# Stick-breaking heads without a mask in the logits: ones in the running product, ones and zeros on the weights

## The chip, the cores and the metric

The kernel runs on one core of a Trainium2 chip. The metric is the device time of one execution in microseconds: three runs of the kernel before took 705.34, 706.74 and 708.4 us, so its median is 706.74 us. Five engines work side by side, each on its own list of instructions in a fixed order: TensorE (PE: matmuls, whose stationary operand is loaded by PEld), VectorE (DVE), ScalarE (ACT), GpSimd (POOL) and SyncE (SP, which issues DMAs). An engine that waits for another holds up all that stands behind the waiting instruction on its own list.

## The reference

One decoder layer on 512 tokens of width 1024: an attention stage with two kinds of heads, a gated feed-forward stage with a short convolution, a gated embedding stage, and a last norm. The change concerns the eight stick-breaking heads, each of width 64:

```
past  = key_pos < q_pos                                  # strictly earlier keys
z     = (q @ k.T) * scale
log_not = where(past, log_sigmoid(-z), 0)
between = reverse_cumsum(log_not) - log_not              # keys between s and t
w     = where(past, exp(log_sigmoid(z) + between), 0)    # weight of key s for query t
out   = w @ v
```

So a weight is sigmoid(z) times the product of sigmoid(-z) over the later keys that the query sees. Keys that it doesn't see must count as 1 in the product and as 0 in the weights.

## The kernel before

Tokens lie in four blocks of 128 queries. Every projection is computed in three matmuls of 512 columns (`mm3`, lines 121 to 123) from operands that are split into a high and a low part; ACT makes the high part of a weight tile (`whi`, line 140) and DVE the low one (`wlo`, line 141). The attention stage takes the stick-breaking heads in four pairs, pair 0 to pair 3, and then the four differential heads. A generator for each pair yields between its steps, and a table `plan` in `stages` says how many units of projection work (three matmuls each) PE does between one step of a pair and the next. These units are the cover under which DVE and ACT work on the pair. PE's order is the order in which the code is written; ACT, DVE and POOL are ordered by a scheduler, by priorities and its own estimates.

A pair's logits fill three PSUM tiles `z`, called groups here by the `g` of `sb_sticks`: group 0 holds query block 3 (512 keys), group 1 blocks 2 and 0 (384 and 128 keys), group 2 block 1 (256 keys), each for both heads. `logits` (line 482) writes them, and at line 490 adds -1e30 at unseen keys of the diagonal block by a matmul of the identity with a mask, two per group. `sb_sticks` then has ACT write sigmoid(-z) into `cum` (line 514) and sigmoid(z) into `beta` (line 515); DVE runs the product backwards over the keys (the scan, line 521) and multiplies `beta` with it (line 522). Because of the mask, sigmoid(-z) is 1 and sigmoid(z) is 0 at unseen keys. The second operand of the scan, `fresh`, has a 1 where a new row of keys begins: the maximum with it starts the product anew.

`pair_out` then transposes the weights block by block on PE (line 566), into which the weights of all three groups go, the first block being one of group 2. Two engines split the result (lines 535 and 536), and PE multiplies with the values (line 578). Between these steps DVE also has: `qkt` (line 377), which evicts a projection from PSUM, the low parts `q` and `k` (line 379), `wlo`, and in pair 1 the values' low part `v_sb` (line 501), which frees the four PSUM buffers `mm` of the value projection. Of `mm` there are four buffers, of `z` two.

Of the kernel before, what the change touches and what calls it, by code (L numbers as in the profile page):

```python
# [11 lines left out]
F32 = mybir.dt.float32  # L12
F32R = mybir.dt.float32r
AF = mybir.ActivationFunctionType
ALU = mybir.AluOpType
# [3 lines left out]
P = 128  # L19
T = 512  # L20
# [13 lines left out]
NEG = -1e30  # L34
# [7 lines left out]
class Kern:  # L42
# [121 lines left out]
    def consts(self):  # L164
        nc, a = self.nc, self.a
        c = self.cpool = self.open("consts")
        self.small = self.open("small", bufs=2)
        self.wraw = self.open("wraw", bufs=2)
        self.wsp = self.open("wsp", bufs=3)
        self.dram = self.open("dram", space=DRAM)  # L170
        su = self.su = self.open("setup", side="right")

        nc.scalar.preload_act_table_set("natural_log_exp_and_others")
        self.ident = c.tile([P, P], F32, name="ident")
        make_identity(nc, self.ident)
        self.ones = c.tile([P, P], F32, name="ones")
        nc.gpsimd.memset(self.ones, 1.0)
        self.mhalf = c.tile([P, 8], F32, name="mhalf")
        nc.gpsimd.memset(self.mhalf, -0.5)
        self.identR = c.tile([P, P], F32R, name="identR")  # L180
        nc.vector.tensor_copy(self.identR, self.ident)
        zero = su.tile([P, P], F32, name="zero")
        nc.gpsimd.memset(zero, 0.0)
        msk = su.tile([P, P], F32, name="msk")

        nc.gpsimd.affine_select(msk, zero, pattern=[[-1, P]], compare_op=ALU.is_gt, fill=NEG, base=0, channel_multiplier=1)
        self.maskR = c.tile([P, P], F32R, name="maskR")
        nc.vector.tensor_copy(self.maskR, msk)

    def params_attn(self, pst):  # L190
        nc, c = self.nc, self.cpool
# [277 lines left out]
            self.nc.vector.tensor_add(self.hT[nt], ps, self.hT[nt])  # L469


    def logits(self, q, k, blocks, mask=False):


        nc = self.nc
        z = self.psz()
        for at, (tb, col) in enumerate(blocks):
            n = (tb + 1) * P
            for i, (x, y) in enumerate(((0, 1), (1, 0), (0, 0))):
                for h in range(2):  # L480
                    o = slice(h * HD, (h + 1) * HD)
                    nc.tensor.matmul(  # L482
                        z[:, h, col : col + n], lhsT=q[o, x, tb * P : (tb + 1) * P], rhs=k[o, y, :n],
                        start=i == 0 and at == 0, stop=i == 2 and at == len(blocks) - 1 and not mask, skip_group_check=True,
                    )
        if mask:

            d = [col // P + tb for tb, col in blocks]
            for h in range(2):
                nc.tensor.matmul(  # L490
                    z[:, h, :].rearrange("p (a b) -> p a b", b=P)[:, d[0] : d[-1] + 1, :], lhsT=self.identR,
                    rhs=self.maskR.unsqueeze(1).to_broadcast([P, len(d), P]), start=False, stop=True, skip_group_check=True,
                )
        return z

    def evict_v(self, tb, ps):
# [7 lines left out]
    def sb_sticks(self, z, g):  # L504


        nc = self.nc
        w = 2 * P if g == 2 else T
        n = 2 * w
        beta = self.slot("beta", "wc" if g == 2 else "w")  # L510
        c = self.cum[g % 2]
        off = 2 * T - n
        two = lambda t: t.rearrange("p (a b) -> p a b", a=2)
        nc.scalar.activation(two(c[:, off : 2 * T]), z[:, :, :w], AF.Sigmoid, scale=-1.0)  # L514
        nc.scalar.activation(two(beta), z[:, :, :w], AF.Sigmoid)

        for c0 in range(off, 2 * T, T):
            back = c[:, c0 : c0 + T][:, ::-1]
            r0 = (3 - g) * P
            fresh = self.fresh[:, r0 : r0 + T] if g else self.fresh[:, 0:1].to_broadcast([P, T])  # L520
            nc.vector.tensor_tensor_scan(back, back, fresh, 1.0, op0=ALU.mult, op1=ALU.max)  # L521
        nc.vector.tensor_mul(beta, beta, c[:, off + 1 : 2 * T + 1])
        for h in range(2):
            b = beta[:, h * w : (h + 1) * w]
            if g == 0:
                self.at[h, 3] = b
            elif g == 1:
                self.at[h, 2], self.at[h, 0] = b[:, : 3 * P], b[:, 3 * P :]
            else:
                self.at[h, 1] = b  # L530
# [8 lines left out]
    def pair_steps(self, pair):  # L539

        q, k = self.qks.pop(pair)
        self.at = {}
        zs = [self.logits(q, k, ((3, 0),), True), self.logits(q, k, ((2, 0), (0, 3 * P)), True)]
        for g in range(2):
            self.sb_sticks(zs[g], g)
        yield
        self.sb_sticks(self.logits(q, k, ((1, 0),), True), 2)
        yield
        yield from self.pair_out(pair, self.v[0])

# [152 lines left out]
    def stages(self):  # L703
        nc, a, tc = self.nc, self.a, self.tc
# [20 lines left out]
        zs = [self.psz(), self.psz()]  # L725
# [66 lines left out]
        for t in self.cum:  # L792
            nc.gpsimd.memset(t[:, 2 * T :], 1.0)

        self.fresh = self.work.tile([P, 6 * P], F32, name="fresh", bufs=1)
        nc.gpsimd.memset(self.fresh, 0.0)
        nc.gpsimd.memset(self.fresh[:, 3 * P : 3 * P + 1], 1.0)
        self.v[0] = self.vp.tile([P, NB, 2 * T], F32R, tag="v", name="v_sb")

        for evict in self.late:  # L800
# [13 lines left out]
        for i in range(2):  # L814
            vd, b = self.vd[:, 2 * i : 2 * i + 2, :], slice(2 * i, 2 * i + 2)
# [66 lines left out]
        for n, (ft, gv) in enumerate(tiles):  # L882
            c, i = divmod(ft, 2)
# [66 lines left out]
        for nh in range(2):  # L950
# [11 lines left out]
            for tb in range(NB):  # L962
                last = nh == 1 and tb == NB - 1
                n = T // 2 if last else T
                for c0 in range(0, T, n):
                    cs = slice(c0, c0 + n)
                    ps = self.psm()[:, :n]
                    for k in range(KT):
                        w = tuple(x[:, k % 2, cs] for x in sp[k // 2])
# [4 lines left out]
                    h = h2n[tb][:, nh * T + c0 : nh * T + c0 + n]  # L974
# [60 lines left out]
```

## Time and profile before

| | |
|---|---|
| median of three runs | 706.74 us (705.34 to 708.4) |
| the profiled execution | 706.04 us, of which its span is 704.3 us |
| TensorE (PE) busy | 684.6 us, 97% of the span |
| VectorE (DVE) busy | 443.1 us, 63% |
| ScalarE (ACT) busy | 315.3 us, 45% |
| GpSimd (POOL) busy | 42.5 us, 6% |
| mean granted TensorE clock | 0.991 of 2.4 GHz |

The span is cut into instructions of each engine with their start and length. In a row of the timeline the first number is the start in us from the span's start, the second the length; "x6" merges six equal instructions, and the bracket at the end gives the time that the engine stood idle ahead of it and what ended that. Consecutive instructions overlap a little in the records, so the cost of one among others is read from start to start. A long matmul's record is longer than its share of PE's time for the same reason. The granted clock is 1.00 at 2.4 GHz and 0.50 at 1.2 GHz. Pair 0 lies at 38 to 62 us, pair 1 at 62 to 97, pair 2 at 102 to 128 and pair 3 at 130 to 156; the differential heads follow to about 240 us.

### The profile page before, as it was taken

How to read it: one execution, taken by the hardware profiler on the slowest of the kernel's cores; microseconds unless marked ns; L12 is line 12 of the kernel's file. 1: busy time of each engine (PE TensorE's matmuls, PEld its weight loads, DVE VectorE, ACT ScalarE, POOL GpSimd, SP SyncE). 2: the span in 40 equal slices, each digit the busy share in tenths (PEclk: the TensorE clock that was granted, in tenths of full speed). 3: DMA queues.
4: the chain of work that ended last, by engine and by line, in shares of the span. 5: the costliest groups of instructions: out<-in, count | busy, mean ns of one | idle time of the engine just before them, and what ended most of it. 6: DMA issues, size and time to landing. Idle time of an engine off the chain costs nothing. (4 is left out here: it accounts for less than half of the span.)

```text
span 704.3 us, 8234 instructions
## 1 busy us (share of the span) xinstructions
PE 684.6 (97%) x3263; PEld 561.2 (80%) x3263; DVE 443.1 (63%) x671; ACT 315.3 (45%) x465; POOL 42.5 (6%) x52
## 2 busy tenths in 40 slices
PE   7999999999999999999999999999999999999995
PEld 6777878787888887888888888888888888888885
DVE  5567669668676768498777777677734232437345
ACT  4565445556554543365444444444423232327422
POOL 2200000000100024100000000000000020202001
PEclk9899999999999999999999999999999999999998
DMA  9423135242226111223322233321323133127002
GB/s 285 158 74 99 60 111 189 60 118 80 76 87 210 60 60 61 87 93 121 119 72 91 77 120 119 95 85 60 126 98 105 60 104 120 41 95 252 17 27 93
DMA packets 66809, 71.64 MB, mean 102 GB/s; under 512 B 2360, under 2 KB 55850, under 8 KB 66771
## 3 DMA queue, kind: packets, MB, share of 16 engines
q1 hardware_dynamic: 63376, 64.76, 28.9%
q10 hardware_dynamic: 2755, 4.27, 1.7%
q0 software_dynamic: 640, 2.10, 0.8%
q8 instruction: 25, 0.41, 0.2%
q14 instruction: 13, 0.11, 0.0%
HBM read 66.90 MB, written 6.84 MB: 105 GB/s over the span
## 5 line engine op out<-in xcount | busy, mean ns | idle before, releaser
L140 ACT CAST whi<-wraw 128x1024 fp32r<-128x1024 f32 (+1 forms) x102 | 105.8, 1037 | 155.1 <-PE mm L122 125.1
L141 DVE TENSOR_TENSOR wlo<-wraw,whi 128x1024 fp32r<-128x1024 f32 (+1 forms) x102 | 123.5, 1211 | 75.0 <-ACT whi L140 73.8
L121 PE MATMUL mm<-xgh,whi 128*128 128x512 f32 x128 | 53.8, 420 | 1.5 <-ACT xgh L330 1.5
L122 PE MATMUL mm<-xgl,whi 128*128 128x512 f32 x128 | 51.5, 402 | 2.0 <-DVE xgl L331 2.0
L860 DVE TENSOR_TENSOR vpad<-mm,rb 128x512 f32<-128x512 f32 x44 | 30.1, 689 | 33.7 <-PE mm L123 33.6
L123 PE MATMUL mm<-xgh,wlo 128*128 128x512 f32 x128 | 51.0, 399 | 0.0
L689 POOL TENSOR_TENSOR sqacc<-sqacc,sq 128x512 f32<-128x512 f32 x14 | 23.1, 1652 | 359.0 <-issue 254.9
L862 ACT ACTIVATE y<-vpad,par,par 128x512 f32<-128x512 f32 x44 | 35.6, 816 | 2.7 <-DVE vpad L860 2.5
L864 DVE SCALAR_TENSOR_TENSOR y<-vpad,par,y 128x512 f32<-128x512 f32 x44 | 33.1, 752 | 1.3
L863 DVE SCALAR_TENSOR_TENSOR y<-vpad,par,y 128x512 f32<-128x512 f32 x44 | 32.8, 748 | 0.0
L121 PEld LDWEIGHTS mm<-xgh,whi 128*128 128x128 f32 x128 | 24.7, 193 | 8.1 <-ACT xgh L330 2.3
L122 PEld LDWEIGHTS mm<-xgl,whi 128*128 128x128 f32 x128 | 24.7, 193 | 8.0 <-DVE xgl L331 3.9
L866 ACT ACTIVATE y<-y 128x512 f32<-128x512 f32 x22 | 13.9, 633 | 34.9 <-DVE y L864 34.9
L123 PEld LDWEIGHTS mm<-xgh,wlo 128*128 128x128 f32 x128 | 24.6, 192 | 5.3
L521 DVE TENSOR_TENSOR_SCAN cum<-cum,fresh 128x512 f32<-128x512 f32 x20 | 23.6, 1213 | 5.5 <-ACT cum L514 5.5
L121 PE MATMUL mm<-whi,xgh 128*128 128x512 f32 x64 | 25.5, 398 | 0.0
L123 PE MATMUL mm<-whi,xgl 128*128 128x512 f32 x64 | 25.0, 390 | 0.0
L122 PE MATMUL mm<-wlo,xgh 128*128 128x512 f32 x64 | 25.0, 390 | 0.0
L626 ACT ACTIVATE pr<-pr,nmx 128x512 f32<-128x512 f32 (+3 forms) x32 | 17.7, 555 | 12.6 <-DVE nmx L622 12.4
L482 PE MATMUL z<-k,q 64*128 64x512 f32 (+3 forms) x192 | 20.3, 335 | 2.8 <-DVE k L379 1.7
L482 PEld LDWEIGHTS z<-k,q 64*128 64x128 f32 x192 | 15.2, 185 | 8.5 <-issue 4.6
L536 DVE TENSOR_TENSOR twl<-z,twh 128x1024 fp32r<-128x1024 f32 (+2 forms) x20 | 18.5, 953 | 5.2 <-ACT twh L535 5.0
(537 smaller groups left out, 1762.9 us busy)
## 6 DMA issues: line engine op xcount, KB each, us to landing
wraw<-in_w_up SPq DMA_DIRECT2D x22, 1024.0 KB, 5.1
wraw<-in_w_in SPq DMA_DIRECT2D x16, 512.0 KB, 5.2
wraw<-in_w_down SPq DMA_DIRECT2D x8, 1024.0 KB, 5.0
wraw<-in_w_in SPq DMA_DIRECT2D x4, 1024.0 KB, 6.0
wraw<-in_w_o SPq DMA_DIRECT2D x4, 1024.0 KB
wraw<-in_w_ple_gate SPq DMA_DIRECT2D x4, 1024.0 KB, 7.2
wraw<-in_w_down SPq DMA_DIRECT2D x4, 768.0 KB, 4.3
sk<-sk ACTq DMA_DIRECT2D x1, 2560.0 KB
```

Of the source, the lines that this page charges most:

```text
L121: nc.tensor.matmul(ps, lhsT=l[0], rhs=r[0], start=start, stop=False, **kw)
L122: nc.tensor.matmul(ps, lhsT=l[0], rhs=r[1], start=False, stop=False, **kw)
L123: nc.tensor.matmul(ps, lhsT=l[1], rhs=r[0], start=False, stop=stop, **kw)
L140: nc.scalar.copy(hi, raw)
L141: nc.vector.tensor_sub(lo, raw, hi.bitcast(F32))
L482: nc.tensor.matmul(z[:, h, col : col + n], lhsT=q[o, x, tb * P : (tb + 1) * P], rhs=k[o, y, :n], start=i == 0 and at == 0, stop=i == 2 and ...
L521: nc.vector.tensor_tensor_scan(back, back, fresh, 1.0, op0=ALU.mult, op1=ALU.max)
L689: nc.gpsimd.tensor_add(sqacc, sqacc, sq)
L860: nc.vector.tensor_mul(u[:, 2 : T + 2], ps, rb2)
L862: nc.scalar.activation(y, u[:, 2 : T + 2], AF.Identity, scale=self.cw(2, ch), bias=self.g("cb", ch))
L863: nc.vector.scalar_tensor_tensor(y, u[:, 1 : T + 1], self.cw(1, ch), y, op0=ALU.mult, op1=ALU.add)
L864: nc.vector.scalar_tensor_tensor(y, u[:, 0:T], self.cw(0, ch), y, op0=ALU.mult, op1=ALU.add)
```

## The change

The mask matmuls of line 490 go, 24 in all: two for each of three groups in each of four pairs. The operand of the scan is a new tile `whole`, which is 1 at every unseen key and not only where a row begins; since the product is at most 1, the maximum with 1 keeps it at 1 there. The scan of group 2 is cut in two of 256 elements, one for each head. After the product DVE multiplies the diagonal blocks of `beta` with `keep`, a triangle of ones and zeros: 128 columns of each head in groups 0 and 2, 256 in group 1. The constants are made by other POOL instructions, and DVE's cast of the mask goes.

```diff
@@ consts
-        zero = su.tile([P, P], F32, name="zero")
-        nc.gpsimd.memset(zero, 0.0)
-        msk = su.tile([P, P], F32, name="msk")
-        nc.gpsimd.affine_select(msk, zero, pattern=[[-1, P]], compare_op=ALU.is_gt, fill=NEG, base=0, channel_multiplier=1)
-        self.maskR = c.tile([P, P], F32R, name="maskR")
-        nc.vector.tensor_copy(self.maskR, msk)
+        self.keep = c.tile([P, P], F32, name="keep")
+        nc.gpsimd.affine_select(
+            self.keep, self.ones, pattern=[[-1, P]], compare_op=ALU.is_gt, fill=0.0, base=0, channel_multiplier=1
+        )
@@ logits
-        if mask:
-            d = [col // P + tb for tb, col in blocks]
-            for h in range(2):
-                nc.tensor.matmul(
-                    z[:, h, :].rearrange("p (a b) -> p a b", b=P)[:, d[0] : d[-1] + 1, :], lhsT=self.identR,
-                    rhs=self.maskR.unsqueeze(1).to_broadcast([P, len(d), P]), start=False, stop=True, skip_group_check=True,
-                )
@@ sb_sticks
-        for c0 in range(off, 2 * T, T):
-            back = c[:, c0 : c0 + T][:, ::-1]
-            r0 = (3 - g) * P
-            fresh = self.fresh[:, r0 : r0 + T] if g else self.fresh[:, 0:1].to_broadcast([P, T])
-            nc.vector.tensor_tensor_scan(back, back, fresh, 1.0, op0=ALU.mult, op1=ALU.max)
+        for c0 in range(off, 2 * T, w):
+            back = c[:, c0 : c0 + w][:, ::-1]
+            r0 = 0 if g == 1 else P
+            nc.vector.tensor_tensor_scan(back, back, self.whole[:, r0 : r0 + w], 1.0, op0=ALU.mult, op1=ALU.max)
         nc.vector.tensor_mul(beta, beta, c[:, off + 1 : 2 * T + 1])
+        diag = two(beta).rearrange("p h (b k) -> p h b k", k=P)[:, :, (3, 2, 1)[g] :, :]
+        nc.vector.tensor_mul(diag, diag, self.keep.unsqueeze(1).unsqueeze(1).to_broadcast(list(diag.shape)))
@@ pair_steps
-        zs = [self.logits(q, k, ((3, 0),), True), self.logits(q, k, ((2, 0), (0, 3 * P)), True)]
+        zs = [self.logits(q, k, ((3, 0),)), self.logits(q, k, ((2, 0), (0, 3 * P)))]
@@ stages
-        self.fresh = self.work.tile([P, 6 * P], F32, name="fresh", bufs=1)
-        nc.gpsimd.memset(self.fresh, 0.0)
-        nc.gpsimd.memset(self.fresh[:, 3 * P : 3 * P + 1], 1.0)
+        self.whole = self.work.tile([P, 5 * P], F32, name="whole", bufs=1)
+        nc.gpsimd.memset(self.whole, 0.0)
+        for b in range(2):
+            w = self.whole[:, b * P : (b + 1) * P]
+            nc.gpsimd.affine_select(w, w, pattern=[[1, P]], compare_op=ALU.is_gt, fill=1.0, base=1 - P, channel_multiplier=1)
```

The scheduler gives DVE another order. On PE, in pair 0's first logits, where `z` is the PSUM tile of a group and `mm` that of a projection, stood before:

```order
L482 MATMUL z_406<-k_369,q_364 128x512 x6
L490 MATMUL z_406<-maskR,identR 128x128 x2
L482 MATMUL z_415<-k_369,q_364 128x384 x6
L482 MATMUL z_415<-k_369,q_364 128x128 x6
L490 MATMUL z_415<-maskR,identR 128x256 x2
L121 MATMUL mm_384<-xgh_264,whi_138 128x512
L122 MATMUL mm_384<-xgl_265,whi_138 128x512
L123 MATMUL mm_384<-xgh_264,wlo_139 128x512
```

and stands now:

```order
L480 MATMUL z_405<-k_368,q_363 128x512 x6
L480 MATMUL z_412<-k_368,q_363 128x384 x6
L480 MATMUL z_412<-k_368,q_363 128x128 x6
L121 MATMUL mm_383<-xgh_258,whi_132 128x512
L122 MATMUL mm_383<-xgl_259,whi_132 128x512
L123 MATMUL mm_383<-xgh_258,wlo_133 128x512
```

The four mask matmuls are gone, as are the two of group 2 a few rows later; nothing else moved on PE, in this pair or any other.

On DVE in pair 0, from the scans of group 1 to the last thing that the pair's transposes need, where `cum` is the running product and `beta` the weights (three of them, one for each group), stood before (line 521 is the scan, 522 the product with it):

```order
L521 SCALAR_TENSOR_TENSOR cum_357<-cum_357,fresh 128x512 x2
L141 TENSOR_TENSOR wlo_451<-wraw_142,whi_450 128x1024
L379 TENSOR_TENSOR q_445<-qkt_446,q_445 128x512
L522 TENSOR_TENSOR beta_436<-beta_436,cum_357 128x1024
L521 SCALAR_TENSOR_TENSOR cum_356<-cum_356,fresh 128x512
L377 SCALAR_TENSOR_TENSOR qkt_494<-mm_454,rb_321 128x512
L522 TENSOR_TENSOR beta_470<-beta_470,cum_356 128x512
L141 TENSOR_TENSOR wlo_499<-wraw_382,whi_498 128x1024
L379 TENSOR_TENSOR k_493<-qkt_494,k_493 128x512
```

and stands now (511 is the scan, 512 the product with it, 514 the new multiplication, 375 and 377 are the old 377 and 379):

```order
L511 SCALAR_TENSOR_TENSOR cum_351<-cum_351,whole 128x512 x2
L514 TENSOR_TENSOR beta_425<-beta_425,keep 128x2x128
L141 TENSOR_TENSOR wlo_448<-wraw_136,whi_447 128x1024
L377 TENSOR_TENSOR q_442<-qkt_443,q_442 128x512
L512 TENSOR_TENSOR beta_432<-beta_432,cum_351 128x1024
L511 SCALAR_TENSOR_TENSOR cum_350<-cum_350,whole 128x256 x2
L375 SCALAR_TENSOR_TENSOR qkt_491<-mm_451,rb_315 128x512
L141 TENSOR_TENSOR wlo_496<-wraw_381,whi_495 128x1024
L514 TENSOR_TENSOR beta_432<-beta_432,keep 128x2x256
L512 TENSOR_TENSOR beta_465<-beta_465,cum_350 128x512
L377 TENSOR_TENSOR k_490<-qkt_491,k_490 128x512
L514 TENSOR_TENSOR beta_465<-beta_465,keep 128x2x128
```

Three multiplications and a scan came in, and the row `wlo` and the row `k`, which stood behind the last write of group 2's weights, now stand ahead of it.

On DVE in pair 2, from the second scan of group 1 on, stood before (its first row holds both scans of the group):

```order
L521 SCALAR_TENSOR_TENSOR cum_357<-cum_357,fresh 128x512 x2
L377 SCALAR_TENSOR_TENSOR qkt_986<-mm_889,rb_321 128x512
L141 TENSOR_TENSOR wlo_991<-wraw_717,whi_990 128x1024
L522 TENSOR_TENSOR beta_973<-beta_973,cum_357 128x1024
L521 SCALAR_TENSOR_TENSOR cum_356<-cum_356,fresh 128x512
L379 TENSOR_TENSOR q_985<-qkt_986,q_985 128x512
L522 TENSOR_TENSOR beta_1007<-beta_1007,cum_356 128x512
L377 SCALAR_TENSOR_TENSOR qkt_1034<-mm_994,rb_321 128x512
L141 TENSOR_TENSOR wlo_1039<-wraw_887,whi_1038 128x1024
L379 TENSOR_TENSOR k_1033<-qkt_1034,k_1033 128x512
```

and stands now, behind the group's first scan and a `qkt`:

```order
L511 SCALAR_TENSOR_TENSOR cum_351<-cum_351,whole 128x512
L514 TENSOR_TENSOR beta_958<-beta_958,keep 128x2x128
L141 TENSOR_TENSOR wlo_984<-wraw_712,whi_983 128x1024
L511 SCALAR_TENSOR_TENSOR cum_350<-cum_350,whole 128x256 x2
L512 TENSOR_TENSOR beta_965<-beta_965,cum_351 128x1024
L377 TENSOR_TENSOR q_978<-qkt_979,q_978 128x512
L512 TENSOR_TENSOR beta_998<-beta_998,cum_350 128x512
L375 SCALAR_TENSOR_TENSOR qkt_1027<-mm_987,rb_315 128x512
L514 TENSOR_TENSOR beta_965<-beta_965,keep 128x2x256
L141 TENSOR_TENSOR wlo_1032<-wraw_882,whi_1031 128x1024
L514 TENSOR_TENSOR beta_998<-beta_998,keep 128x2x128
L377 TENSOR_TENSOR k_1026<-qkt_1027,k_1026 128x512
```

Here the second `qkt` and the second `wlo` came ahead of the last write of group 2's weights, beside the three multiplications and the scan. In pair 1 DVE's other work keeps its place among the old instructions, in pair 3 one `wlo` came ahead.

## Rows read from the trace of the kernel before

**Rows 1.** First part of the page: busy time, share of the span, instructions.

```profile
PE 684.6 (97%) x3263; PEld 561.2 (80%) x3263; DVE 443.1 (63%) x671; ACT 315.3 (45%) x465; POOL 42.5 (6%) x52
```

**Rows 2.** Waits of PE: total us, times, longest us.

```profile
PE z L566 <- DVE beta L522: 2.3, 1, 2.3
```

**Rows 3.** PE, pair 1's logits with masks: start, us, engine, line, operation.

```profile
62.13 0.96 PE L482 MATMUL z<-k,q 64*128 64x512 f32 x6
...
64.96 0.40 PE L122 MATMUL mm<-wlo,xgh 128*128 128x512 f32 x1
...
66.89 0.62 PE L482 MATMUL z<-k,q 64*128 64x256 f32 x6
...
68.00 0.40 PE L122 MATMUL mm<-wlo,xgh 128*128 128x512 f32 x1
```

**Rows 4.** PE, a differential head's logits, which have no masks.

```profile
184.36 1.79 PE L482 MATMUL z<-k,q 64*128 64x512 f32 x18
...
186.42 0.40 PE L122 MATMUL mm<-xgl,whi 128*128 128x512 f32 x1
...
188.20 0.62 PE L482 MATMUL z<-k,q 64*128 64x256 f32 x6 [0.46 <-DVE nmx L622]
...
189.08 0.40 PE L122 MATMUL mm<-xgl,whi 128*128 128x512 f32 x1
```

**Rows 5.** PE in pair 0: last matmul ahead of the transposes, and the transposes.

```profile
51.65 0.39 PE L123 MATMUL mm<-whi,xgl 128*128 128x512 f32 x1
54.31 1.94 PE L566 MATMUL z<-ident,beta 128*128 128x128 f32 x16 [2.27 <-DVE beta L522]
```

**Rows 6.** DVE in pair 0, up to the last write of its weights.

```profile
50.63 1.22 DVE L522 TENSOR_TENSOR beta<-beta,cum 128x1024 f32<-128x1024 f32 x1
51.76 1.22 DVE L521 TENSOR_TENSOR_SCAN cum<-cum,fresh 128x512 f32<-128x512 f32 x1
52.90 0.67 DVE L377 SCALAR_TENSOR_TENSOR qkt<-mm,rb 128x512 f32<-128x512 f32 x1
53.48 0.68 DVE L522 TENSOR_TENSOR beta<-beta,cum 128x512 f32<-128x512 f32 x1
```

**Rows 7.** Groups of DVE by shape: busy us, mean ns, idle before.

```profile
L536 DVE TENSOR_TENSOR twl<-z,twh 128x256 fp32r<-128x256 f32 x4 | 1.7, 416 | 0.0
```

**Rows 8.** DVE in pair 2, and PE's transposes there.

```profile
104.79 2.34 DVE L521 TENSOR_TENSOR_SCAN cum<-cum,fresh 128x512 f32<-128x512 f32 x2 [1.08 <-ACT cum L514]
...
115.33 0.69 DVE L522 TENSOR_TENSOR beta<-beta,cum 128x512 f32<-128x512 f32 x1
...
116.86 1.36 PE L566 MATMUL z<-ident,beta 128*128 128x128 f32 x11
```

**Rows 9.** DVE's first value eviction in pair 1, and PE's next piece.

```profile
75.71 1.41 DVE L501 SCALAR_TENSOR_TENSOR v_sb<-mm,rstd,v_sb 128x512 fp32r<-128x512 f32 x2
...
77.98 0.39 PE L121 MATMUL mm<-xgh,whi 128*128 128x512 f32 x1
```

**Rows 10.** DVE and PE in pair 3, before its transposes.

```profile
141.54 0.69 DVE L522 TENSOR_TENSOR beta<-beta,cum 128x512 f32<-128x512 f32 x1
...
145.18 1.03 PE L566 MATMUL z<-ident,beta 128*128 128x128 f32 x8
```

**Rows 11.** Stretches: length, PE busy (instructions), PEclk, DMA share, GB/s.

```profile
19.00:20.00 1.00, 1.00 (x4) 0.50 0.42 166
...
23.00:24.00 1.00, 1.00 (x8) 0.95 0.08 29
...
52.50:54.30 1.80, 0.00 (x0) 1.00 1.18 319
...
699.00:700.00 1.00, 0.00 (x0) 0.50 0.00 0
```

**Rows 12.** PE: a start after a gap near 18 us, and its last matmul.

```profile
18.48 0.79 PE L122 MATMUL mm<-xgl,whi 128*128 128x512 f32 x1 [0.87 <-DVE xgl L331]
...
696.28 0.28 PE L123 MATMUL mm<-gwh,h27l 128*128 128x256 f32 x1
```

More of the change, by code (lines that the diff above doesn't have):

```diff
@@ L469, in half_out, with logits @@
             self.nc.vector.tensor_add(self.hT[nt], ps, self.hT[nt])
-    def logits(self, q, k, blocks, mask=False):
+    def logits(self, q, k, blocks):
         nc = self.nc
@@ L483, in logits @@
                         z[:, h, col : col + n], lhsT=q[o, x, tb * P : (tb + 1) * P], rhs=k[o, y, :n],
-                        start=i == 0 and at == 0, stop=i == 2 and at == len(blocks) - 1 and not mask, skip_group_check=True,
+                        start=i == 0 and at == 0, stop=i == 2 and at == len(blocks) - 1, skip_group_check=True,
                     )
-        if mask:
-            d = [col // P + tb for tb, col in blocks]
-            for h in range(2):
-                nc.tensor.matmul(
-                    z[:, h, :].rearrange("p (a b) -> p a b", b=P)[:, d[0] : d[-1] + 1, :], lhsT=self.identR,
-                    rhs=self.maskR.unsqueeze(1).to_broadcast([P, len(d), P]), start=False, stop=True, skip_group_check=True,
-                )
         return z
@@ L546, in pair_steps @@
         yield
-        self.sb_sticks(self.logits(q, k, ((1, 0),), True), 2)
+        self.sb_sticks(self.logits(q, k, ((1, 0),)), 2)
         yield
```

## The prediction

> **What bounds the kernel now.** I read the shares of the engines first, then what TensorE (PE) waits for, then the instructions around each pair of stick-breaking heads on PE and on VectorE (DVE), and last the clock. PE is busy for 97% of the span [rows 1], so a microsecond taken off its list is worth a microsecond unless a wait takes its place, and every microsecond for which PE stands still is lost. In the stick-breaking stage PE waits once for the weights `beta`, for 2.3 us [rows 2]. That is pair 0: PE's last projection matmul starts at 51.65 and ends at 52.04, and the transposes start at 54.31 [rows 5], 0.15 us after DVE ended the product of group 2, at 53.48 + 0.68 = 54.16 [rows 6]. There DVE bounds the kernel and not PE. In pair 2 the same product ends at 115.33 + 0.69 = 116.02, and PE comes at 116.86 [rows 8]: 0.84 us to spare. In pair 3 it ends at 142.23, and PE comes at 145.18 [rows 10]: 2.95 us to spare. In pair 1 a longer stretch of projection work stands ahead of the transposes, so the weights are not what matters there.
>
> **What the change takes off PE.** The differential heads have the same logits without masks, so they show what remains. From the first logits matmul to the second projection matmul behind them, pair 1 takes 64.96 - 62.13 = 2.83 us for groups 0 and 1 and 68.00 - 66.89 = 1.11 for group 2 [rows 3]; a differential head takes 186.42 - 184.36 = 2.06 and 189.08 - 188.20 = 0.88 [rows 4]. The difference, 0.77 + 0.23 = 1.0 us, is what a pair's six mask matmuls cost PE: 4.0 us in all, if PE keeps it.
>
> **What it adds on DVE.** From start to start a product of 1024 elements takes 51.76 - 50.63 = 1.13 us (and so does a `wlo` of that size), a scan of 512 takes 52.90 - 51.76 = 1.14, and 512 elements of another kind take 53.48 - 52.90 = 0.58 [rows 6], with 0.6 as a round figure. A two-operand instruction of 256 elements has a record of 0.416 us [rows 7], of which some 0.09 overlaps with the next, as in the others: 0.33. So the multiplications by `keep` are estimated at 0.33 (group 0), 0.6 (group 1) and 0.33 (group 2), 1.26 us for a pair. No row shows one with an operand repeated by a stride of zero, so I keep as ends 0.7 us for a pair (about half) and 2.3 (each as an instruction of twice the elements). No row shows a scan of 256 either. Two of them cost at least the 1.14 of one of 512 and at most 2.28; I take 1.2, since the fixed part of the other kinds is small (0.33 for 256, 0.58 for 512).
>
> The order weighs more than these. In pair 0 the scheduler now puts a `wlo` (1.13) and the `k` (0.6) ahead of the last write of group 2's weights; in pair 2 it is a `qkt` (0.6) and a `wlo`, in pair 3 a `wlo`. All of these stood behind that write before. Behind the write stand PE's transposes, and with PE's fixed order all projections of the kernel behind these.
>
> **The sum, pair by pair.** Pair 0: 0.33 + 0.06 + 1.13 + 0.6 + 0.6 + 0.33 = 3.05 us more on DVE. I take no earlier start of its scans from the masks, because DVE first has a reduction that waits for a DMA. So the transposes start at 57.36, 3.05 later; PE is there at 51.04, and the 1.0 us that it saved is spent in the wait, which grows from 2.27 to 6.3 us.
>
> Pair 1: DVE gets 0.33 + 0.06 + 0.6 + 0.33 + 0.1 (group 2's multiplication stands right behind the product that it needs) = 1.4 us more ahead of the first `v_sb`, and starts 0.38 earlier, half of the 0.77. That `v_sb` ended at 75.71 + 0.75 = 76.46 and will end at 77.5. It frees the PSUM buffer that PE's next piece takes, and PE is there at 77.98 - 1.0 = 76.98 [rows 9]. About 0.5 us of the saving is kept, 0.5 lost in a new wait.
>
> Pair 2: 0.33 + 0.06 + 0.6 + 0.6 + 1.13 + 0.33 = 3.05 more, 0.38 earlier. The last write ends at 116.02 + 2.67 = 118.7, the transposes start at 118.85 instead of 116.86: 2.0 us lost, with a gap of 3.0 us, as PE is there at 115.86.
>
> Pair 3: 0.33 + 0.06 + 0.6 + 1.13 + 0.33 = 2.45 more, 0.38 earlier: the weights are ready at 142.23 + 2.07 + 0.15 = 144.45. PE keeps 0.38 + 0.23 = 0.6 of its 1.0 (the second `z` tile waits for an eviction by DVE in this pair) and comes at 144.6. No wait, by a margin of 0.1; 0.6 gained.
>
> Together 3.05 - 0.5 + 2.0 - 0.6 = 3.95 us more. The ends of the unknown costs change pair 0 and pair 2 by -0.6 to +2.1 us each. Nothing behind the pairs gives it back: PE has work at once from there on, and DVE and ACT work from what PE hands them. The start is counted at nothing: the constants are needed only in pair 0, and the cast of the mask lies in time when DVE waits.
>
> **The clock.** A gap also has an after-effect. PE's gap of 2.27 us in pair 0 left the granted clock at 1.00 [rows 11]. At the kernel's end PE's last matmul ends at 696.56 [rows 12], and from 699 the clock is at 0.50 [rows 11], so it had fallen no later than 2.4 us after. In the start-up PE took up steady work at 18.48 [rows 12] at 0.50 (1.2 GHz) and got 1.00 (2.4 GHz) only at 23.1 (the mean of 0.95 in the stretch from 23 to 24 is 0.1 us at half) [rows 11]: 4.6 us at half speed, in which 2.3 us of PE's work is lost. After a gap of 6.3 us I expect the fall, at this price; its ends are nothing and 3.1 us (a third more, since one case shows no spread). After the 3.0 us of pair 2, which lies just above the gap that cost nothing and the time that sufficed at the end, I take half of 2.3, 1.15, with ends nothing and 2.3. The Trainium skill, "TensorE: Matmul & The Clock Gate", in "HAM oscillation — how this bites in real kernels", has the rule that idle gaps between groups of matmuls send the clock back to half, so that the work behind each begins slow. It speaks against this change; by it both gaps would pay in full, and without it neither. The trace bears it out at the kernel's end and not in the gap of pair 0.
>
> So the forecast is 706.04 + 3.95 + 2.3 + 1.15 = 713.4 us, made against the profiled execution, whose 706.04 lies 0.7 below the median of the runs, inside their spread. I leave it at 713.4, 0.9% above that median. Its own range is 711.5 to 715.
>
> **Rivals.** 1. The gaps come, and the clock stays: 706.04 + 3.95 = 710.0. For it speaks the gap in pair 0 of the kernel before; against it that the gap nearly triples. Chance 0.17. 2. The clock falls in both gaps, at 3.1 and 2.3 us: 715.4. For it speaks the fall at the kernel's end within 2.4 us; against it that pair 2 has only 3.0. Chance 0.23. 3. Faster: the multiplications and the moved work vanish in DVE's idle time, and PE keeps what it saves: 706.04 - 3.6 = 702.4. The place is the last write of group 2's weights in pairs 0 and 2, and it decides if DVE gets there no later than before. For it speaks that DVE is idle 37% of the time. Against it, DVE is already what PE waits for in pair 0, and its new work stands between the logits and the transposes, with 0.84 us to spare in pair 2 against 2.67. It would need `wlo`, `k` and `qkt` to cost nothing there. Chance 0.05.
>
> **How the numbers follow.** The forecast has 0.53, the rivals 0.17, 0.23 and 0.05, and 0.02 is left for anything else. A measurement can tell 0.5% from no change, 3.5 us around 706.7. Rival 1 lies at that edge, so about half of it and a little of the rest count as no change: same 0.12; faster 0.04; slower 0.84. The range goes from 709.6, where the clock costs nothing, to 716.5, where it costs all and the unknown multiplications a little more.
>
> **What would show it.** In the profile after, PE should have two waits of the transposes for `beta`, about 6.3 us at 51 us and 3.0 us in pair 2, a wait of about half a microsecond for `v_sb` in pair 1, and none in pair 3. The multiplications should take 0.4 and 0.7 us and a scan of 256 about 0.7. The granted clock should read 0.50 for some 4 us from about 57 us on. The logits of a pair should take PE 1.0 us less. I am wrong if DVE reaches the last write sooner than 56 us, if the clock stays at 1.00, or if a wait in a later stage shrinks by what the pairs lose.

## The result and the profile after

The changed kernel takes 713.45 us (median of 8 runs, 710.56 to 716.11), the kernel before, on the same chip, 706.40 us (8 runs, 705.23 to 708.40). The ratio is 1.0095, with an interval of 1.0076 to 1.0114: slower by 0.95%, where 713.4 us was forecast. The profiled execution took 711.63 us, of which the span is 709.9.

The first part of the page, as in [rows 1]:

```profile
PE 681.5 (96%) x3239; PEld 558.5 (79%) x3239; DVE 447.6 (63%) x686; ACT 315.1 (44%) x465; POOL 42.7 (6%) x52
```

PE has 24 instructions and 3.1 us less, DVE 15 instructions and 4.5 us more, and the span is 5.6 us longer. PE's own list got shorter, so what made the kernel longer are waits of PE. Its list of waits (total us, times, longest us) says where the time went, beside the one wait of [rows 2]:

```profile
PE z L558 <- DVE beta L514: 8.4, 2, 5.5
...
PE z L480 <- DVE av L577: 1.0, 1, 1.0
PE z L480 <- ACT beta L505: 0.9, 1, 0.9
...
PE mm L121 <- DVE v_sb L491: 0.3, 1, 0.3
```

The transposes (now line 558) wait for the weights twice and not once, 8.4 us in place of 2.3. PE's timeline shows the places, in the order of time: group 2's logits in pair 0, its transposes (as [rows 5]), pair 1's logits (as [rows 3]), the projection behind `v_sb` (as [rows 9]) and pair 2's transposes (as [rows 8]).

```profile
42.40 0.62 PE L480 MATMUL z<-k,q 64*128 64x256 f32 x6 [0.89 <-ACT beta L505]
...
51.02 0.39 PE L123 MATMUL mm<-whi,xgl 128*128 128x512 f32 x1
...
66.45 1.78 PE L480 MATMUL z<-k,q 64*128 64x512 f32 x18
...
68.50 0.40 PE L122 MATMUL mm<-wlo,xgh 128*128 128x512 f32 x1
...
81.76 0.50 PE L121 MATMUL mm<-xgh,whi 128*128 128x512 f32 x1 [0.29 <-DVE v_sb L491]
...
122.75 1.94 PE L558 MATMUL z<-ident,beta 128*128 128x128 f32 x16 [2.84 <-DVE beta L514]
```

In pair 0 PE's last projection ends at 51.02 + 0.39 = 51.41, and the transposes start at 56.95. DVE's timeline up to there, as [rows 6]:

```profile
51.69 1.27 DVE L511 TENSOR_TENSOR_SCAN cum<-cum,whole 128x256 f32<-128x256 f32 x2
52.87 0.67 DVE L375 SCALAR_TENSOR_TENSOR qkt<-mm,rb 128x512 f32<-128x512 f32 x1
53.45 1.22 DVE L141 TENSOR_TENSOR wlo<-wraw,whi 128x1024 fp32r<-128x1024 f32 x1
54.59 0.69 DVE L514 TENSOR_TENSOR beta<-beta,keep 128x512 f32<-128x512 f32 x1
55.19 0.68 DVE L512 TENSOR_TENSOR beta<-beta,cum 128x512 f32<-128x512 f32 x1
55.79 0.69 DVE L377 TENSOR_TENSOR k<-qkt,k 128x512 fp32r<-128x512 f32 x1
56.39 0.42 DVE L514 TENSOR_TENSOR beta<-beta,keep 128x256 f32<-128x256 f32 x1
```

The transposes start 0.14 us after the last multiplication by `keep` ends, at 56.81, and between the scans and that end stand a `wlo` and a `k` that the transposes don't need. The clock, in stretches as [rows 11]:

```profile
53.00:54.00 1.00, 0.00 (x0) 0.00 (x0) 1.00 (x2) 0.43 (x1) 0.00 (x0) 0.76 1.19 316
54.00:56.00 2.00, 0.00 (x0) 0.00 (x0) 2.00 (x4) 0.19 (x1) 0.00 (x0) 0.50 0.55 131
...
58.00:60.00 2.00, 2.00 (x12) 2.00 (x11) 0.03 (x1) 1.01 (x1) 0.00 (x0) 0.50 0.00 0
60.00:61.00 1.00, 1.00 (x6) 0.92 (x5) 1.00 (x1) 0.43 (x1) 0.00 (x0) 0.83 0.00 0
...
122.00:123.00 1.00, 0.25 (x3) 0.28 (x3) 1.00 (x3) 0.00 (x0) 0.00 (x0) 1.00 0.97 281
```

The granted clock (third number from the end) fell to 0.50 about 53.5, 2.1 us after PE stopped, and was back at 60.3, 3.4 us after it had taken up work. In pair 2's gap, of 2.84 us, it stayed at 1.00.

Pieces that both traces have show where the time came from. Each number is the start in this trace less the start in the trace of before:

| place | after - before, us | step |
|---|---|---|
| pair 0 logits | -0.53 | start-up |
| pair 0 transposes | +2.64 | +3.17 |
| pair 1 logits | +4.32 | +1.68, in which the clock was at 0.50 |
| behind the projection that waits for `v_sb` | +3.78 | -0.54 |
| pair 2 logits | +3.90 | +0.12 |
| pair 2 transposes | +5.89 | +1.99 |
| first differential head's logits | +5.41 | -0.48 |
| end | +5.6 | +0.19 |

### The profile page after: what moved, and what is told of

Its sections match the earlier page's. It is cut to its first block, busy times and chain, and to the rows that moved or that the text cites. A ratio compares the mean times of both kernels' runs of the same rounds, so it can differ in the third digit from the quotient of the medians.

```text
span 709.9 us, 8201 instructions
## 1 busy us (share of the span) xinstructions
PE 681.5 (96%) x3239; PEld 558.5 (79%) x3239; DVE 447.6 (63%) x686; ACT 315.1 (44%) x465; POOL 42.7 (6%) x52
## 5 line engine op out<-in xcount | busy, mean ns | idle before, releaser
L511 DVE TENSOR_TENSOR_SCAN cum<-cum,whole 128x512 f32<-128x512 f32 (+1 forms) x24 | 24.0, 1034 | 4.5 <-ACT cum L504 4.5
L527 ACT CAST twh<-z 128x1024 fp32r<-128x1024 f32 (+2 forms) x20 | 15.3, 804 | 20.3 <-PE z L558 13.2
```

Source lines behind the costliest of these rows:

```text
L511: nc.vector.tensor_tensor_scan(back, back, self.whole[:, r0 : r0 + w], 1.0, op0=ALU.mult, op1=ALU.max)
```

## The experiments

The theory: the time is set by when DVE ends the last write of group 2's weights in pairs 0 and 2, and part of the delay there comes from the scheduler's order; the clock adds to it. Rivals: PE's masks or the multiplications themselves count, or GpSimd or more cover could take them. All ratios are to the kernel before, timed on the same chip. The price of the clock in pair 0 is read in each trace from PE's first transpose there to the first logits matmul of pair 1: the kernel before, whose clock stayed at 1.00, takes 62.13 - 54.31 = 7.82 us for it, the changed kernel 66.45 - 56.95 = 9.50.

**e1_nokeep: no multiplications.** The two lines of `keep` go, so that the weights at unseen keys are not set to zero.

```diff
-        diag = two(beta).rearrange("p h (b k) -> p h b k", k=P)[:, :, (3, 2, 1)[g] :, :]
-        nc.vector.tensor_mul(diag, diag, self.keep.unsqueeze(1).unsqueeze(1).to_broadcast(list(diag.shape)))
```

> The changed kernel without its multiplications by keep (weights at unseen keys stay as they are: that part of the computation is left out); the order of VectorE's other instructions in the pairs is the same. Theory A (VectorE's list ahead of the transposes in pairs 0 and 2 sets the loss, order and multiplications together, and the clock adds to it): both waits shrink by 1.26 us, to about 4.3 and 1.6 us, the clock still falls in pair 0 and no longer in pair 2: about 709.5 us against 713.4 of the changed kernel. Rival B (the multiplications alone are the loss, the moved wlo, k and qkt cost nothing): the waits go back to about 2.3 and 0, and the time below that of the kernel before, about 703 us.

Measured: 705.54 us (12 runs), ratio 0.9987 (0.9967 to 1.0006). Neither number: the theory's 709.5 is 4 us too high, the rival's 703 too low. PE in pair 0:

```profile
55.45 1.94 PE L556 MATMUL z<-ident,beta 128*128 128x128 f32 x16 [3.79 <-DVE beta L512]
```

Without the multiplication the last write is the product, and `k` in pair 0 and `qkt` and `wlo` in pair 2 stand behind it again; only the `wlo` in pair 0 stays ahead. The edit undid most of the order too, which the expectation overlooked. It shows that all of the loss goes with the multiplications and the order that they bring, and not how it splits.

**e2_order: only the order.** All of the change stays; DVE's `wlo` and `k` in pair 0 and `qkt` and `wlo` in pair 2 are held behind the last write of the weights.

```diff
+LATE_SPLIT = (6, 14)
+LATE_EVICT = ((1, 1, 1), (3, 1, 0), (3, 1, 1))
...
+            with self.behind(self.nsplit in LATE_SPLIT):
+                nc.vector.tensor_sub(lo, raw, hi.bitcast(F32))
...
+        return self.tc.issue_after(self.last) if late else nullcontext()
```

> The changed kernel with VectorE's order mended: in pair 0 one wlo and the k, in pair 2 the second qkt and the second wlo are queued behind the last multiplication by keep, where they stood behind the last write of the weights before. Nothing is left out. Theory A: the wait of pair 0 falls by 1.73 us to 3.8, that of pair 2 by 1.73 to 1.1, and the clock no longer falls in pair 2: about 708.8 us. Rival B (only the multiplications cost): no change, 713.4 us.

Measured: 708.74 us (12 runs), ratio 1.0025 (1.0007 to 1.0043), as expected. PE in pair 0, at pair 1's logits and in pair 2:

```profile
55.48 3.64 PE L568 MATMUL z<-ident,beta 128*128 128x128 f32 x16 [3.99 <-DVE beta L523]
...
65.66 1.78 PE L489 MATMUL z<-k,q 64*128 64x512 f32 x18
...
120.11 1.94 PE L568 MATMUL z<-ident,beta 128*128 128x128 f32 x16 [1.10 <-DVE beta L523]
```

The waits shrink from 5.54 and 2.84 to 3.99 and 1.10 us. So by the medians 4.7 of the 7 us of the loss (713.45 - 708.74 of 713.45 - 706.40) come from the order, what it does to the clock included; by the profiled executions, in both of which the clock fell in pair 0, it is 711.63 - 708.77 = 2.9 of 5.6. Behind the rest stand the multiplications and the scan, less what PE is spared, and the clock where it still falls: here it costs 65.66 - 55.48 = 10.18 less 7.82, so 2.36 us, most of the 2.7 by which this execution is behind the profiled one of the kernel before.

**e3_busy: only the clock.** Matmuls that nothing needs fill the gaps, 45 in pair 0 and 20 in pair 2.

```diff
+BUSY = {0: 45, 2: 20}
...
+            for _ in range(BUSY.get(pair, 0) if b == 0 else 0):
+                nc.tensor.matmul(ps[:, :P], lhsT=self.identR, rhs=self.identR, start=True, stop=True)
```

> The changed kernel with 45 and 20 small matmuls of constants (128 columns, about 0.11 us each: 5.1 and 2.3 us) on TensorE in the gaps of pairs 0 and 2, ahead of the transposes. They end inside the gaps, so the waits stay where they were. Theory A: the clock stays at 1.00, the 16 transposes of pair 0 take 1.9 us instead of 3.6, and the time is that of the gaps alone, about 710 us, with less spread between runs. Rival C (the clock's falls cost nothing, since PE has time to catch up): 713.4 us. If the 45 matmuls end too late, pair 0 gets longer than in the changed kernel, by what they overrun.

Measured: 710.00 us (11 runs, 709.51 to 711.23), ratio 1.0047 (1.0030 to 1.0065), as expected. PE in pair 0 and at pair 1's logits:

```profile
51.10 5.13 PE L556 MATMUL z<-identR 128*128 128x128 f32 x45
56.99 1.94 PE L561 MATMUL z<-ident,beta 128*128 128x128 f32 x16 [0.76 <-DVE beta L515]
...
64.81 1.78 PE L481 MATMUL z<-k,q 64*128 64x512 f32 x18
```

The transposes start at 56.99, as late as with the change alone (56.95), and the median is 3.45 us lower. About half of that is seen in the traces: to pair 1's logits PE takes 64.81 - 56.99 = 7.82 us again, 1.68 less than in the changed kernel, whose profiled execution paid nothing in pair 2. That the clock makes the other half too, in the longer runs of the changed kernel, isn't shown. No trace of such a run is kept, and the mean granted clock of its runs doesn't follow their time: 0.992 at 712.35 us, 0.990 at 715.03, and 0.987 at the 711.63 of the profiled one. The profiled execution of e3 is the slowest of its eleven, and its clock fell 1.6 us after the end of a wait of only 1.71 us, for the first differential head's `k`:

```profile
167.23 1.83 PE L481 MATMUL z<-k,q 64*128 64x512 f32 x18 [1.71 <-DVE k L378]
```

```profile
167.00:169.00 2.00, 1.77 (x19) 1.65 (x19) 0.85 (x4) 0.03 (x1) 0.00 (x0) 0.95 0.00 0
169.00:170.00 1.00, 1.00 (x4) 0.83 (x3) 0.54 (x2) 1.00 (x3) 0.00 (x0) 0.50 0.00 0
```

**e4_before_nomask: only PE's saving.** The kernel before without its 24 mask matmuls, so without masking.

```diff
-        if mask:
+        if False:
```

> The kernel before without its mask matmuls (unseen keys are not masked: that part is left out), with no multiplication in their place. Its scheduler also puts the wlo of pair 0 ahead of the product of group 2. Theory A: pairs 1, 2 and 3 gain 1.0, 1.0 and 0.6 us, pair 0's transposes start 1.1 us later for the wlo, and the wait there, 2.3 before, is about 4.4 us, long enough for the clock to fall (1.7 us): about 706 us, no gain. Rival D (what PE is spared is gained everywhere): 702.4 us.

Measured: 707.23 us (12 runs), ratio 1.0001 (0.9984 to 1.0019): no gain, as the theory has it, 1.2 us above its number. DVE in pair 0, and PE there, at pair 1's logits and at the first differential head's:

```profile
41.41 2.33 DVE L521 TENSOR_TENSOR_SCAN cum<-cum,fresh 128x512 f32<-128x512 f32 x2
...
52.35 1.22 DVE L141 TENSOR_TENSOR wlo<-wraw,whi 128x1024 fp32r<-128x1024 f32 x1
53.48 0.68 DVE L522 TENSOR_TENSOR beta<-beta,cum 128x512 f32<-128x512 f32 x1
```

```profile
36.99 1.78 PE L482 MATMUL z<-k,q 64*128 64x512 f32 x18
...
54.31 2.61 PE L566 MATMUL z<-ident,beta 128*128 128x128 f32 x16 [3.58 <-DVE beta L522]
...
63.74 1.78 PE L482 MATMUL z<-k,q 64*128 64x512 f32 x18
...
162.46 1.76 PE L482 MATMUL z<-k,q 64*128 64x512 f32 x18 [1.71 <-DVE k L379]
```

That the transposes start at 54.31, to the hundredth where they started in [rows 5], is chance. DVE's scans start 1.16 us earlier here than before (41.41 against 42.57), and the `wlo` of 1.13 that the scheduler put ahead of the product takes that back. The wait grew from 2.27 to 3.58 us, where 4.4 were expected, and the clock fell: to pair 1's logits PE takes 63.74 - 54.31 = 9.43 us, 1.61 more than before. From there to the first differential head's logits it takes 162.46 - 63.74 = 98.72 us, and before 163.46 - 62.13 = 101.33: the 2.6 us expected of pairs 1 to 3 are gained. So PE keeps what it is spared there, and pair 0 spends it again, 1.03 us by the order (17.32 us from its logits to its transposes, 16.29 before) and 1.61 by the clock. The rival of 702.4 is refuted for this order of DVE's; no run has the kernel before without its masks in the old order.

**e5_plan_after and e6_plan_before: more cover.** Projection work moves into the two gaps, in the changed kernel and in the one before: four units each, those of pair 0 from pair 1, those of pair 2 from the end of pair 3.

```diff
-        plan = [(0, 0, 3), (0, 1, 12), (0, 2, 4), (0, 3, 4), (1, 0, 3), (1, 1, 18), (0, 4, 4), (1, 2, 4), (1, 3, 4), (1, 4, 4)]
+        plan = [(0, 0, 3), (0, 1, 16), (0, 2, 4), (0, 3, 4), (1, 0, 3), (1, 1, 14), (0, 4, 4), (1, 2, 4), (1, 3, 4), (1, 4, 4)]
...
-            plan += [(p, 0, 3), (p, 1, 13), (p, 2, 4), (p, 3, 4), (p, 4, 4 if p == 2 else 9)]
+            plan += [(p, 0, 3), (p, 1, 17 if p == 2 else 13), (p, 2, 4), (p, 3, 4), (p, 4, 4 if p == 2 else 5)]
```

> The changed kernel with another plan of the cover: 16 units instead of 12 ahead of pair 0's transposes and 14 instead of 18 in pair 1, 17 instead of 13 in pair 2 and 5 instead of 9 at the end of pair 3; a unit is 0.68 us of TensorE's work. VectorE's order in pairs 0 and 2 is that of the changed kernel. Theory A: the gap of pair 0 shrinks by 2.7 us to about 2.8 and the clock falls seldom, the gap of pair 2 shrinks to about 0.1: 2.7 + 1.7 + 2.7 + 1.8 us less than 713.4, about 704.5 us, below the kernel before. Rival E (the cover is missed where it is taken away, in pair 1 and pair 3): 710 us or more.

> The kernel before with the same plan of the cover (16, 14, 17, 5). Theory A: it has only the 2.3 us of pair 0 to gain, and the clock's rare falls there: about 703.5 us, so that with enough cover on both sides the change is worth no more than the difference to the changed kernel with this plan, about +1 us. Rival E: slower than 706 us.

Measured: 710.25 us (6 runs), ratio 1.0052 (1.0034 to 1.0070), and 709.30 us (12 runs), ratio 1.0038 (1.0024 to 1.0053). Both miss; the kernel before even becomes slower. PE in e5_plan_after:

```profile
54.24 0.50 PE L121 MATMUL mm<-whi,xgh 128*128 128x512 f32 x1 [2.35 <-DVE qkt L375]
57.60 1.94 PE L558 MATMUL z<-ident,beta 128*128 128x128 f32 x16 [0.35 <-DVE beta L514]
...
79.46 0.50 PE L121 MATMUL mm<-xgh,whi 128*128 128x512 f32 x1 [1.75 <-DVE v_sb L491]
...
165.42 2.35 PE L480 MATMUL z<-k,q 64*128 64x512 f32 x18 [3.69 <-DVE k L377]
```

The waits for `beta` are nearly gone, and others stand in their place. In pair 0 the added work needs a PSUM buffer that DVE's `qkt` frees, in the same busy stretch of DVE. The four units taken from pair 3 had covered the first differential head's `k`: PE's wait for it grew from 1.71 to 3.69 us, and the clock fell there, to 0.50 from 167 to 169 us. In e6 PE waits 1.64 us for `qkt` in pair 0 and the same 3.69 for `k`, where the clock fell too. Cover was moved, not made.

**e7_plan_order: both edits**, the plan of e5 and the order of e2.

> The changed kernel with the plan of the cover (16, 14, 17, 5) and VectorE's order mended in pairs 0 and 2 (moved wlo, k and qkt behind the last multiplication). Theory A: pair 0's gap is about 1.2 us, no other: about 703 us. Rival E: 709 us or more.

Measured: 709.05 us (8 runs), ratio 1.0043 (1.0025 to 1.0061). A miss for the same reason: PE waits 2.3 us for `qkt` in pair 0 and 3.7 for `k`, as in e5.

**e8_pool: the multiplications on GpSimd**, ahead of the product.

```diff
-        nc.vector.tensor_mul(beta, beta, c[:, off + 1 : 2 * T + 1])
-        nc.vector.tensor_mul(diag, diag, self.keep.unsqueeze(1).unsqueeze(1).to_broadcast(list(diag.shape)))
+        nc.gpsimd.tensor_mul(diag, diag, self.keep.unsqueeze(1).unsqueeze(1).to_broadcast(list(diag.shape)))
+        nc.vector.tensor_mul(beta, beta, c[:, off + 1 : 2 * T + 1])
```

> The changed kernel with the multiplications by keep on GpSimd and ahead of the product: beta is multiplied there as soon as ScalarE has written it, while VectorE runs the scans. VectorE's list is then that of the run without the multiplications (705.5 us), and nothing is left out. Theory A: waits as in that run, 3.8 us in pair 0 and none in pair 2, about 705.7 us. Rival F (GpSimd's work on SBUF slows VectorE's instructions at its side): up to 3.3 us longer in pairs 0 and 2 each, 707 to 713 us.

Measured: 712.48 us (6 runs), ratio 1.0081 (1.0061 to 1.0101), the rival's number. DVE and GpSimd in pair 0:

```profile
46.91 1.21 DVE L511 TENSOR_TENSOR_SCAN cum<-cum,whole 128x512 f32<-128x512 f32 x1
48.04 2.25 DVE L511 TENSOR_TENSOR_SCAN cum<-cum,whole 128x512 f32<-128x512 f32 x1
50.22 1.69 DVE L141 TENSOR_TENSOR wlo<-wraw,whi 128x1024 fp32r<-128x1024 f32 x1
```

```profile
47.28 1.93 POOL L513 TENSOR_TENSOR beta<-beta,keep 128x512 f32<-128x512 f32 x1 [3.16 <-ACT beta L505]
```

The first scan takes its usual 1.21 us; the second, which comes up while GpSimd multiplies, has a record of 2.25, and the `wlo` behind them, beside GpSimd's next multiplication, 1.69 instead of 1.22. The 2.25 fit a second scan that began its work only when GpSimd ended: 47.28 + 1.93 = 49.21, and 49.21 + 1.14 = 50.35, where the next instruction starts at 50.22. The Trainium skill, "SBUF — State Buffer", in "SBUF: two separate sides", says of VectorE and GpSimd that they share a pair of ports, and that of an instruction of VectorE with two inputs from SBUF and one of GpSimd the one that starts first has it until it ends; the trace agrees within 0.13 us. PE now waits 5.74 us for the weights in pair 0, longer than with the change alone, and 1.42 in pair 2.

**e9_difference, e10_before_late, e11_difference_late, e12_difference_late_busy: a version without the bound.** The weight of a key is the running product behind it less the one with it, so one subtraction takes the place of sigmoid(z), product and `keep` (e9, in the order of e2). And in pair 0 of the kernel before the first scan stands behind a reduction for the differential heads, which waits for a DMA:

```profile
42.42 0.23 DVE L233 CUSTOM_DVE_ANT_0 mix4l<-mix4l 128x64 f32<-128x64 f32 x1 [1.92 <-DMA mix4l<-in_lambda_k]
...
42.57 2.34 DVE L521 TENSOR_TENSOR_SCAN cum<-cum,fresh 128x512 f32<-128x512 f32 x2
```

e10 moves that reduction behind pair 3, in the kernel before. e11 does both, e12 fills what is left of the gap.

```diff
-        nc.scalar.activation(two(beta), z[:, :, :w], AF.Sigmoid)
...
-        nc.vector.tensor_mul(beta, beta, c[:, off + 1 : 2 * T + 1])
+            last = nc.vector.tensor_sub(beta, c[:, off + 1 : 2 * T + 1], c[:, off : 2 * T])
...
+        with self.tc.issue_after(self.last):
+            self.lam()
```

> The weight of a key is the running product after it less the running product with it, so DVE subtracts neighbours of `cum` where it multiplied `beta` with `cum`. Sigmoid(z), the multiplications by `keep` and `keep` itself aren't needed: at an unseen key both products are 1. A last column of each row is set to zero. The order is that of e2_order: `wlo` and `k` of pair 0, `qkt` and `wlo` of pair 2 behind the last write of the weights. Theory A (what counts is when DVE ends the last write of the weights): e1_nokeep without the one `wlo` of 1.13 us ahead of that write, and three small instructions more, so the transposes of pair 0 start about 54.4 instead of 55.45, PE's wait there is about 2.8 us, none in pair 2; span about 702.1 where e1_nokeep had 703.1, median about 704.8, from 703.8 in an execution whose clock stays at 1.00 to 705.5 in one where it falls. Rival (the subtraction by rows of 511 and 255 elements or the small writes cost more than the product, or the next wait in pair 1 takes it all): 706 to 707.

> The kernel before, with the two reductions of lambda, their exponent and `neglam` moved from pair 0 to behind pair 3's weights. In pair 0 DVE's first scan waits for the second reduction, and that for a DMA that lands at 41.97; ACT loads a table for the exponent and one back between the sigmoids of groups 0 and 1. Theory A: the scans of pair 0 start about 1.2 us earlier (at the end of ACT's first sigmoid, about 41.4 instead of 42.57), the transposes too, PE's wait of 2.27 us there shrinks to about 1.1; median about 705 (a gap that short should leave the clock alone), 0.2% below before. Rival: ACT's sigmoid of group 1 is what DVE then waits for, or the exponent comes late for the first differential head: 706.

> e9_difference and the move of e10_before_late together. Theory A: the transposes of pair 0 start about 53.2, PE's wait there is about 1.7 us, the clock stays at 1.00; the median about 703 (702.5 to 703.8), below both kernels, and its runs lie within 2 us. Rival (what pair 0 gains turns into PE's waits in pair 1 for `v_sb` or for the first differential head's `k`): 704.8 as e9_difference.

> e11_difference_late, with 14 matmuls of 128 columns that nothing needs written into the first tile of pair 0's transposes ahead of these: by e3_busy (45 took 5.13 us) they fill 1.6 of PE's 2.65 us gap and delay nothing. Theory A (the spread of e11_difference_late, 702.57 to 707.61, comes from the clock, which fell in that gap in its profiled execution): the clock stays at 1.00 in pair 0, the transposes start as in e11_difference_late at about 52.9, the median is about 702.7 and the runs lie within 2 us. Rival (the spread comes from elsewhere, the DMA or a later gap): median about 704.7, spread 4 to 5 us as there.

Measured, with the longest waits of PE in the stick-breaking stage and ahead of the first differential head:

| kernel | median us | lowest to highest | ratio (interval) | waits, us |
|---|---|---|---|---|
| before | 705.90 | 704.97 to 709.38 | 1 | 2.27, 1.71 |
| e9_difference | 707.84 | 706.30 to 708.32, and one of 1849.41 | 1.0019 (1.0007 to 1.0030) | - |
| e10_before_late | 705.34 | 704.22 to 706.25 | 0.9987 (0.9976 to 0.9998) | 1.46, 1.71 |
| e11_difference_late | 704.75 | 702.57 to 707.61 | 0.9982 (0.9969 to 0.9995) | 2.65, 1.71 |
| e12_difference_late_busy | 702.89 | 700.09 to 703.24 | 0.9934 (0.9911 to 0.9956) | 1.12, 1.71 |

e9 missed by 3 us, and its profiled execution, of 1849 us, gives nothing to read; why it is that far above e11 stays open. Its other eleven runs have a mean granted clock of 0.988 to 0.990, like the changed kernel's profiled execution (0.987), which speaks for a fall in each of them and doesn't show it. e10 hit: its scans start at 40.96, its transposes at 52.58. e11 missed its 703 by 1.7 and its spread by 3; e12 was run to see why. PE in the two:

```profile
52.90 3.25 PE L575 MATMUL z<-ident,beta 128*128 128x128 f32 x16 [2.65 <-ACT k L387]
...
62.01 1.78 PE L492 MATMUL z<-k,q 64*128 64x512 f32 x18
```

```profile
49.89 1.67 PE L573 MATMUL z<-identR 128*128 128x128 f32 x14
...
52.68 1.94 PE L578 MATMUL z<-ident,beta 128*128 128x128 f32 x16 [1.12 <-DVE beta L531]
...
60.46 1.78 PE L493 MATMUL z<-k,q 64*128 64x512 f32 x18
```

In e11 the clock fell in a gap of 2.65 us, and the transposes took 3.25 us; with the gap filled they take 1.94, and the median is 1.9 us lower, as expected. The two ran on different chips, so the traces are the better evidence: to pair 1's logits PE takes 62.01 - 52.90 = 9.11 us in e11 and 60.46 - 52.68 = 7.78 in e12, which is 1.33 of the 1.55 us between the profiled executions (703.36 and 701.81). Eight of the nine runs of e12 lie between 701.81 and 703.24, the ninth at 700.09, where all were expected within 2 us. It beats both kernels. The kernel before took 708.18 us beside it (13 runs, 704.55 to 709.93); against its 705.90 in the table's first row the gain of e12 is 0.4% and not 0.66.

## Why the prediction was right

The likeliest case came, with its waits at the places named. Step by step:

- **What bounds the kernel.** Right: where DVE ends last, in pair 0, a shorter list of PE's buys nothing, and where PE waits for nothing it buys what it saves. e4 shows both, 2.6 us gained in pairs 1 to 3 and as much lost in pair 0.
- **Masks, 1.0 us a pair.** From the first logits matmul of pair 1 to the second projection matmul behind it PE now takes 68.50 - 66.45 = 2.05 us, as forecast (2.06). In pair 0 little of it became a longer wait of the transposes: PE came earlier to group 2's logits and waited 0.89 us for ACT's sigmoid there, a wait that the prediction doesn't name. It cost nothing, since DVE set the end of pair 0; it is most of why the gap was 5.54 us and not 6.3.
- **Multiplications and scans.** They take 0.42 and 0.69 us in the rows of DVE above, where 0.4 and 0.7 were forecast; two scans of 256 take 52.87 - 51.69 = 1.18 from start to start, where 1.2 was taken. The operand repeated by a stride of zero costs nothing more: plain operands of these sizes have 0.416 [rows 7] and 0.68 [rows 6].
- **Moved work.** e2 shows it to be the largest part of the loss: 4.7 of 7 us by the medians, 2.9 of 5.6 by the profiled executions.
- **The start.** Counted at nothing, and rightly: pair 0's logits start 0.53 us earlier here than in the trace of before, but between 36.99 (e4) and 38.66 (e7) in those of the other kernels, and at 38.11 in e5, which differs from the change only in the plan: that much differs from execution to execution.
- **The pairs.** Forecast +3.05, -0.5, +2.0, -0.6; in the table of places +3.17, -0.54, +1.99, -0.48. The wait for `v_sb` was 0.29 us, for a forecast of 0.5.
- **The clock.** Forecast 2.3 and 1.15. The profiled execution paid 1.68 in pair 0 and nothing in pair 2, so the sum, which was made against the profiled 706.04, is 1.8 us above the profiled 711.63, and nearly all of that lies here. The 2.3 is at the upper end of what a fall in pair 0 cost in the traces: 1.29 (e11), 1.36 (e8), 1.61 (e4), 1.68 and 2.36 us (e2). By the medians filling both gaps is worth 713.45 - 710.00 = 3.45 us (e3), the same as 2.3 + 1.15. That these agree, and with them the median and the forecast to 0.05 us, is partly luck: a price that some executions pay and others don't was put in as half, and half of the 3.45 isn't traced to the clock. The rule of the Trainium skill, "TensorE: Matmul & The Clock Gate", "HAM oscillation — how this bites in real kernels", that a wait of PE that is long enough sends the clock back, held in pair 0 and not, in this execution, in pair 2. The Trainium skill makes it depend on the length of the wait, which the prediction's "both gaps would pay in full" leaves out.

## What to carry to other kernels

An edit that saves time on the busiest engine is worth what the waits behind it leave: ask first which engine ends last at the next meeting point, and price there every instruction that the scheduler puts ahead of it, moved ones above all. A gap of the matmul engine can cost twice, once as a gap and once, in some executions, as a fall of its clock, here 1.3 to 2.4 us; matmuls that nothing needs removed the second part here (e3, e12). Before cover is moved into a gap, look for what it had covered, and for the buffer that it needs.

## What the runs showed of the hardware

In the profiled executions the clock fell in gaps of PE, or up to 1.6 us behind their end: in those of 2.65 (e11), 3.69 (e6, e7), 3.99 (e2), 5.54 (the change) and 5.74 us (e8), and behind those of 1.71 (e3), 2.33 (e7), 3.58 (e4) and 3.69 us (e5). It stayed at 1.00 with gaps of 2.27 (before), 2.35 (e5), 2.84 (the change, pair 2) and 3.79 us (e1), and with the same wait of 1.71 us for `k` in nine other kernels. So the length of a gap of about 2 to 4 us doesn't decide it alone.

A fall shows in the time of a run in some kernels: the six runs of e7 with a mean granted clock of 0.993 or 0.995 took 708.77 to 709.51 us, the two with 0.985 and 0.986 took 712.38 and 711.76. It doesn't in all: two runs of e11 with 0.995 took 702.57 and 705.79, and two of the kernel before with 0.995, on one chip, 705.24 and 709.09, farther apart than any fall here cost. Kernels without a gap above 2 us have runs within 1.7 (e3), 2.0 (e10) and 3.1 us (e12, eight of its nine within 1.4); the kernel before, the change and e11, with longer ones, spread over 4.4, 5.6 and 5.0, though e5, with 3.69, over 1.6 only. So the clock makes a part of the spread, and what makes the rest stays open.
